# GpSimd's tap additions of a 31-tap causal convolution, issued as 512-column pieces instead of 1024

## The chip, the cores and the metric

The kernel runs on one core of a Trainium2 chip. The metric is the device time of one execution in microseconds (us), lower being better; a kernel's time is the median of its runs. The engines are named as the profile names them: PE (TensorE's matmuls), PEld (its weight loads), DVE (VectorE), ACT (ScalarE), POOL (GpSimd) and SP (the queue from which DMAs are issued).

## The reference

One inference step of a two-layer streaming encoder over 2048 prompt frames and 32 sample frames, model width 1024, in float32. Layer 0 has two branches of 512 channels, layer 1 a token-mixing branch and a stick-breaking attention. The change touches layer 0's branch B, a Conformer convolution module:

```python
proj = xn @ w_in
a_x, a_c, a_b, a_z, b_val, b_glu, b_z = jnp.split(proj, 7, axis=-1)
a_conv, new_a = _causal_dwconv(a_c * a_x, hist_a, a_conv_w)                    # 3 taps
a_out = a_b * a_conv * jax.nn.silu(a_z)
b_conv, new_b = _causal_dwconv(b_val * jax.nn.sigmoid(b_glu), hist_b, b_conv_w) # 31 taps
b_out = jax.nn.silu(_layernorm(b_conv, b_ln_g, b_ln_b)) * jax.nn.silu(b_z)
y = jnp.concatenate([a_out, b_out], axis=-1) @ w_out
```

Each of the 512 channels of branch B is convolved along time with its own 31 taps. All outputs (the streams, the convolution states, keys and values) are float32.

## The kernel before, in words

**Layout.** Features lie on the 128 partitions, time along the columns. The 2080 columns are worked in two halves (1056 with the sample's 32 columns in the first, 1024 in the second), each half in three chunks of 352, 352 and 352 or 320 columns. A branch of 512 channels is four tiles of 128, numbered j.

**Matmuls.** Every float32 product is made of three fp32r products (high x high, high x low, low x high). `split` (lines 172 to 175) makes the two parts: ACT copies the high part (L174), DVE subtracts it from the source (L175). A step of `run_phase` (line 259) is one output tile of one chunk: 24 matmuls into one of three PSUM banks. `wconv` (line 236) splits a tile of weights as two pieces of 512 columns, about one tile for every three steps. The two subtractions L175 (tiles wf, whl) stand behind each other on DVE, and both inputs lie in SBUF.

**Order of the work.** The program's order is fixed when it is built. PE's steps set the pace: four times in each step `tick` (line 145) advances the lanes, queues of generators with a rate each, and what a lane yields between two ticks goes into the engines' queues there. Each engine then works through its own queue in order.

**Layer 0's input phase** (`l0_in`, line 606) runs once for each half, and the convolutions run as lanes beside its 84 steps. The tiles of branch B are shared out. Tiles 1 and 3 are made on DVE (`conv_b_dve`, line 662): one multiply-add per tap over all columns (L672) with the accumulator in PSUM. Tiles 0 and 2 are made by ACT and GpSimd (`conv_b_pool`, line 681): for each tap ACT multiplies the shifted input by the tap's weight into a buffer `cvt` (L692, two buffers), and GpSimd adds the buffer to the tile's row of R (L694). `pieces(30)` (line 657) gives the column ranges: in the first half 1024 columns of the prompt and 32 of the sample, in the second half 1024 columns alone. So the first half has two adds for each tap and the second has one; 30 taps x 2 tiles make 60 taps in each half. ACT's next product into a buffer waits until GpSimd has read it.

**What stands beside it.** DVE also does the short convolution of branch A (`conv_a`, line 699: L704 and L709, all operands in SBUF) and reads most PSUM banks (L747, L761, L771, L775); PE's step three later needs the bank that is read. GpSimd also keeps the convolutions' states (L647, L651), multiplies R by the gate (L773, which waits for DVE's zz, L771), and, when both of its tiles are done, does the sums of branch B's layer norm (`layernorm`, line 793: L801 to L803), for whose result PE's matmul L808 waits.

Of the kernel before, what the change touches and what calls it, by code (L numbers as in the profile page):

```python
# [85 lines left out]
class Build:  # L86
# [519 lines left out]
    def l0_in(self, half):  # L606
        nc, I, O = self.nc, self.I, self.O
        ph = 0 if half == 0 else 3
        R = q = None
# [3 lines left out]
        NP = 1024  # L613

        def begin():
            nonlocal R, q
            if half == 0:
                self.xst.close()
                self.R = self.rst2.enter_context(self.tc.tile_pool(
                    name="l0", bufs=1, side="right", reuse_waits="tile")).tile([P, 8, 1056], F32, name="R0")  # L620
            R = self.R
            q = self.lp = cst.enter_context(self.tc.tile_pool(name="conv", bufs=1, reuse_waits="tile"))
            self.on512 = q.tile([P, P], F32, name="on512")
            nc.gpsimd.memset(self.on512, 1.0 / 512)
            nonlocal dve
            dve = self.lane(0.5, *(conv_b_dve(j) for j in (1, 3)))
            self.lane(0.35, *(conv_b_pool(j) for j in (0, 2)))
            for c in HC[half]:
                self.lane(0.25, ln_b(c, 3 * (c % 3)))
            self.prep(self.prep_sbuf(ph + 1, half, "cat"))  # L630
# [26 lines left out]
        def pieces(hist):  # L657
            if half == 0:
                return [(0, NP, 0), (hist + NP, hist + NP + 32, NP)]
            return [(0, NP, 0)]  # L660
# [20 lines left out]
        def conv_b_pool(j):  # L681
            while ("u", j) not in self.ready:
                yield
            u = U[j]
            n = NP + 62 if half == 0 else NP
            wb = K_CB + 31 * j
            for a, b, d in pieces(30):
                nc.scalar.activation(R[:, 4 + j, d : d + b - a], u[:, a:b], AF.Copy, scale=self.kc[:, wb : wb + 1])
            yield
            for t in range(1, 31):  # L690
                f = q.tile([P, NP + 62], F32, tag="cv", name="cvt", bufs=2)
                nc.scalar.activation(f[:, :n], u[:, t : t + n], AF.Copy, scale=self.kc[:, wb + t : wb + t + 1])  # L692
                for a, b, d in pieces(30):
                    nc.gpsimd.tensor_add(R[:, 4 + j, d : d + b - a], R[:, 4 + j, d : d + b - a], f[:, a:b])  # L694
                yield
            self.ready.add(("conv", j))
            yield
# [927 lines left out]
```

## Time and profile before

| | us |
|---|---|
| median of 3 runs (2697.5 to 2699.49) | 2698.99 |
| the profiled execution | 2703.41 |
| its span | 2701.7 |
| PE busy in the span | 2602.0 (96%) |
| DVE busy | 1712.7 (63%) |
| ACT busy | 1280.8 (47%) |
| POOL busy | 990.7 (37%) |
| the adds L694, 180 of them | 322.4 |

Everything in the profile is of the one profiled execution, whose own time lies 4.4 us above the median of the runs. Busy time is that of an engine's instructions; a busy share over the whole span hides stretches in which an engine is full. A line of the trace that groups instructions gives their count, busy time and mean duration, and then the idle time of the engine just before them and what ended it. A duration holds also the time in which an instruction that has begun is held up. L694 is line 694 of the kernel.

### The profile page before, as it was taken

To read this page: it belongs to the slowest core of one execution; us is meant where nothing else is said; L and a number is where in the kernel's file an instruction comes from. 1 tells how busy PE (TensorE), PEld (TensorE's weight loads), DVE (VectorE), ACT (ScalarE), POOL (GpSimd) and SP (SyncE) were. 2 spreads that over 40 slices of the span, in tenths; PEclk is the share of its full clock that TensorE was granted. 3 is DMA by queue.
4 is the path that set the end of the run, shared out by engine and by line. 5 is a ranking of instruction groups with operands and counts; after the bars stand their busy time and mean duration, and the time that the engine had idled before them with its cause. 6 is when DMAs were issued, how large, how long until landed. Compare 5 with 4: busy or idle time off the path is not lost.

```text
span 2701.7 us, 44677 instructions
## 1 busy us (share of the span) xinstructions
PE 2602.0 (96%) x16738; PEld 2522.4 (93%) x16738; DVE 1712.7 (63%) x2809; ACT 1280.8 (47%) x2348; POOL 990.7 (37%) x883
## 2 busy tenths in 40 slices
PE   7999999999999999999999999998899999998998
PEld 7999999999999999999889999898799899897997
DVE  6697644467986434622242568777788988976344
ACT  5554433445544323432341366666766666753233
POOL 2699712117796001200201044445354343551012
PEclk9999999999999999999999999999999999999998
DMA  5111124331111133455121585543234533324411
GB/s 193 52 45 40 48 85 149 107 111 48 48 43 44 62 106 109 124 197 181 57 78 66 187 250 183 182 128 93 72 95 120 159 109 118 123 83 165 127 60 63
DMA packets 215320, 291.05 MB, mean 108 GB/s; under 512 B 23744, under 2 KB 142144, under 8 KB 215104
## 3 DMA queue, kind: packets, MB, share of 16 engines
q1 hardware_dynamic: 215104, 288.20, 34.0%
q8 instruction: 132, 2.16, 0.3%
q14 instruction: 84, 0.69, 0.1%
HBM read 220.16 MB, written 67.96 MB: 107 GB/s over the span
## 4 chain that ended last, share of the span: by engine, by line
PE 76%; DVE 9%; issue 4%; POOL 4%; DMA 3%; ACT 3%; SPq 1%; DVEq 0%; ACTq 0%; POOLq 0%
PE mm L275 59%; PE o L1249 4%; PE at L1228 4%; POOL R L694 2%; PE ple L287 2%; PE z L1197 2%; PE z L1198 2%; DVE kp L1207 2%; DVE whl L175 1%; DVE op L387 1%; PE mm L534 1%; DMA qt<-qd 1%; PE cm L1058 1%; DVE stg L353 1%; DMA kc<-in_ck 1%
## 5 line engine op out<-in xcount | busy, mean ns | idle before, releaser
L275 PE MATMUL mm<-op,whl 128*128 128x352 f32 (+1 forms) x12672 | 2145.1, 324 | 33.0 <-DVE R L837 8.8
L275 PEld LDWEIGHTS mm<-op,whl 128*128 128x128 f32 x12672 | 2011.7, 189 | 51.1 <-DVE R L837 9.1
L1211 POOL TENSOR_TENSOR bt<-bt,kp 128x512 f32<-128x512 f32 (+2 forms) x320 | 308.0, 965 | 524.9 <-DVE kp L1207 253.1
L175 DVE TENSOR_TENSOR whl<-wf,whl 128x512 fp32r<-128x512 f32 x352 | 304.9, 904 | 154.6 <-ACT whl L174 143.1
L694 POOL TENSOR_TENSOR R<-R,cvt 128x1024 f32<-128x1024 f32 (+1 forms) x180 | 322.4, 1817 | 45.8 <-ACT cvt L692 42.5
L174 ACT CAST whl<-wf 128x512 fp32r<-128x512 f32 x352 | 202.4, 621 | 222.4 <-PE mm L275 176.8
L911 POOL TENSOR_TENSOR acc<-acc,zz 128x352 f32<-128x352 f32 (+1 forms) x78 | 76.8, 984 | 552.5 <-ACT zz L907 552.5
L1203 ACT ACTIVATE kp<-z 128x512 f32<-128x512 f32 (+2 forms) x320 | 171.7, 536 | 223.9 <-PE z L1200 102.3
L1207 DVE TENSOR_TENSOR_SCAN kp<-kp,cr,z 128x513 f32<-128x513 f32 x192 | 245.1, 1277 | 50.3 <-ACT bt L1204 47.9
L692 ACT ACTIVATE cvt<-u,kc 128x1086 f32<-128x1086 f32 (+1 forms) x120 | 140.8, 1178 | 128.1 <-POOL R L694 122.7
L175 DVE TENSOR_TENSOR aT<-at,aT 128x512 fp32r<-128x512 f32 (+1 forms) x288 | 188.7, 656 | 2.0 <-ACT aT L174 2.0
L1249 PE MATMUL o<-aT,vt 128*128 128x256 f32 (+1 forms) x1152 | 185.2, 283 | 0.0
L1228 PE MATMUL at<-ident,bt 128*128 128x128 f32 x1088 | 168.7, 275 | 9.2 <-DVE aT L175 6.2
L1204 ACT ACTIVATE bt<-z 128x512 f32<-128x512 f32 (+2 forms) x320 | 170.1, 532 | 0.0
L174 ACT CAST aT<-at 128x512 fp32r<-128x512 f32 (+1 forms) x288 | 164.5, 571 | 6.9 <-PE at L1228 5.6
L1249 PEld LDWEIGHTS o<-aT,vt 128*128 128x128 f32 x1152 | 164.5, 189 | 0.0
L1228 PEld LDWEIGHTS at<-ident,bt 128*128 128x128 f32 x1088 | 127.5, 141 | 36.5 <-DVE aT L175 7.2
L1207 DVE TENSOR_TENSOR_SCAN kp<-kp,z 128x129 f32<-128x129 f32 (+3 forms) x128 | 104.8, 819 | 84.3 <-ACT bt L1204 83.6
L672 DVE SCALAR_TENSOR_TENSOR acc<-u,kc,acc 128x1086 f32<-128x1086 f32 (+1 forms) x116 | 152.9, 1318 | 2.6
L894 DVE TENSOR_TENSOR sg<-ple,sg 128x352 f32<-128x352 f32 (+1 forms) x72 | 37.1, 515 | 162.0 <-PE ple L287 110.9
L837 DVE TENSOR_TENSOR R<-mm,row 128x352 f32<-128x352 f32 (+1 forms) x96 | 49.5, 516 | 139.9 <-PE mm L275 136.6
L1197 PE MATMUL z<-kt,qt 128*128 128x512 f32 (+2 forms) x320 | 118.3, 370 | 12.7 <-DVE kp L1207 7.7
(188 smaller groups left out, 2218.9 us busy)
## 6 DMA issues: line engine op xcount, KB each, us to landing
wf<-in_win SPq DMA_DIRECT2D x224, 256.0 KB, 3.0
kt<-kd SPq DMA_DIRECT2D x80, 256.0 KB, 4.0
vt<-vd SPq DMA_DIRECT2D x80, 256.0 KB, 3.7
wf<-in_wout SPq DMA_DIRECT2D x64, 256.0 KB, 3.3
wf<-in_wg SPq DMA_DIRECT2D x64, 256.0 KB, 3.1
qt<-qd SPq DMA_DIRECT2D x128, 128.0 KB, 3.4
vd<-vs SPq DMA_DIRECT2D x16, 512.0 KB, 4.3
kd<-hl SPq DMA_DIRECT2D x32, 256.0 KB, 4.0
```

The costliest lines, as they stand in the source:

```text
L174: self.nc.scalar.copy(hi, src)
L175: self.nc.vector.tensor_sub(lo, src, hi.bitcast(F32))
L275: nc.tensor.matmul(ps, wt[:, a, k, :], x[:, b, k, :w], start=(n == 0), stop=(n == 23))
L672: nc.vector.scalar_tensor_tensor(out=acc[:, :n], in0=u[:, t : t + n], scalar=self.kc[:, wb + t : wb + t + 1], in1=acc[:, :n], op0=ALU.mult ...
L694: nc.gpsimd.tensor_add(R[:, 4 + j, d : d + b - a], R[:, 4 + j, d : d + b - a], f[:, a:b])
L1197: nc.tensor.matmul(z[:, :N], qq[:, 0, e * P : e * P + P], kk[:, :N], start=True, stop=False)
L1203: nc.scalar.activation(kp[:, :N], z[:, :N], AF.Sigmoid, scale=-0.125)
L1204: nc.scalar.activation(bt[:, :N], z[:, :N], AF.Sigmoid, scale=0.125)
L1207: nc.vector.tensor_tensor_scan(rev, rev, z[:, 0:1].to_broadcast([P, N + 1]), init, op0=ALU.mult, op1=ALU.bypass)
L1211: nc.gpsimd.tensor_mul(bt[:, :N], bt[:, :N], kp[:, 1 : N + 1])
L1228: nc.tensor.transpose(at[:, off : off + P], bt[:, kb * P : (kb + 1) * P], self.ident)
L1249: nc.tensor.matmul(d, vt[(G, h, c)][:, kb], t[:, l, o0 : o0 + w], start=(c == G and p == 0 and bank == 0 and x == 0 and l == 0), stop=(fin ...
```

## The change

The inner loop of `conv_b_pool` now walks each column range in steps of NP // 2 = 512 columns: the add over 1024 columns becomes two adds over 512, and the 32-column add of the first half stays one. The values added are the same, and ACT's product stays one instruction over all columns. GpSimd has 120 instructions more.

```diff
                 for a, b, d in pieces(30):
-                    nc.gpsimd.tensor_add(R[:, 4 + j, d : d + b - a], R[:, 4 + j, d : d + b - a], f[:, a:b])
+                    for h in range(0, b - a, NP // 2):
+                        e = min(h + NP // 2, b - a)
+                        r = R[:, 4 + j, d + h : d + e]
+                        nc.gpsimd.tensor_add(r, r, f[:, a + h : a + e])
                 yield
```

## Rows read from the trace of the kernel before

**Rows 1.** The page: busy time and share of the span of each engine.
```profile
PE 2602.0 (96%) x16738; PEld 2522.4 (93%) x16738; DVE 1712.7 (63%) x2809; ACT 1280.8 (47%) x2348; POOL 990.7 (37%) x883
```

**Rows 2.** Windows: length; busy PE, PEld, DVE, ACT, POOL; clock; DMA share; GB/s.
```profile
88.00:277.00 189.00, 183.26 (x1131) 182.12 (x1129) 146.79 (x150) 97.93 (x118) 183.24 (x142) 0.99 0.15 46
638.00:807.00 169.00, 161.77 (x1029) 160.99 (x1028) 156.34 (x126) 85.22 (x104) 148.84 (x67) 0.99 0.15 45
```

**Rows 3.** Timeline of PE: start, length, instructions, [idle time before <- what ended it].
```profile
200.44 34.59 PE L275 MATMUL mm<-op,whl 128*128 128x352 f32 x216 [0.63 <-DVE zz L771]
235.77 11.87 PE L275 MATMUL mm<-op,whl 128*128 128x352 f32 x72 [0.74 <-DVE prod L761]
250.71 25.00 PE L275 MATMUL mm<-op,whl 128*128 128x352 f32 x144 [3.07 <-DVE zz L771]
277.02 0.86 PE L808 MATMUL stat<-l,on 128*128 128x352 f32 x2 [1.31 <-POOL l L803]
...
731.43 22.61 PE L275 MATMUL mm<-op,whl 128*128 128x352 f32 x144 [1.06 <-DVE prod L761]
755.92 22.58 PE L275 MATMUL mm<-op,whl 128*128 128x352 f32 x144 [1.88 <-DVE R L775]
782.79 17.46 PE L275 MATMUL mm<-op,whl 128*128 128x352 f32 x100 [4.29 <-DVE prod L761]
```

**Rows 4.** Windows behind two of PE's stops; the granted clock stands third from last.
```profile
250.70:254.10 3.40, 3.39 (x11) 3.39 (x12) 3.40 (x4) 1.25 (x2) 3.37 (x2) 0.51 0.00 0
...
782.80:786.20 3.40, 3.40 (x13) 3.40 (x14) 3.37 (x4) 2.54 (x3) 3.32 (x2) 0.56 0.00 0
```

**Rows 5.** Groups of POOL by shape, 223.9 to 231.3 us: busy us, mean ns.
```profile
L694 POOL TENSOR_TENSOR R<-R,cvt 128x1024 f32<-128x1024 f32 x3 | 7.2, 2404 | 0.0
L694 POOL TENSOR_TENSOR R<-R,cvt 128x32 f32<-128x32 f32 x3 | 0.7, 236 | 0.0
```

**Rows 6.** Timeline of POOL, first half (three taps) and second half (four).
```profile
223.71 7.73 POOL L694 TENSOR_TENSOR R<-R,cvt 128x32 f32<-128x32 f32 x6
...
728.43 9.86 POOL L694 TENSOR_TENSOR R<-R,cvt 128x1024 f32<-128x1024 f32 x4
```

**Rows 7.** Groups of POOL by shape, whole span: the two that work on 512 columns.
```profile
L1211 POOL TENSOR_TENSOR bt<-bt,kp 128x512 f32<-128x512 f32 x224 | 247.4, 1104 | 305.9 <-DVE kp L1207 156.4 <-DVE kp L1188 118.5 <-PE at L1228 15.7
...
L1268 POOL TENSOR_TENSOR fo<-fo,dz 64x512 f32<-64x512 f32 x32 | 41.3, 1290 | 22.6 <-DVE fo L1267 14.9 <-POOL bt L1211 5.1 <-issue 1.2
```

**Rows 8.** Groups of POOL by shape, 90 to 277 us, with the idle time before.
```profile
L694 POOL TENSOR_TENSOR R<-R,cvt 128x1024 f32<-128x1024 f32 x60 | 151.4, 2524 | 9.7 <-ACT cvt L692 9.7
...
L773 POOL TENSOR_TENSOR R<-R,zz 128x352 f32<-128x352 f32 x6 | 8.5, 1423 | 0.9 <-DVE zz L771 0.9
...
L651 POOL COPY keep_a<-prod 128x2 f32<-128x2 f32 x3 | 1.0, 349 | 1.4 <-DVE prod L761 1.4
```

**Rows 9.** Timeline of POOL: the first tap of the first half.
```profile
88.78 4.97 POOL L694 TENSOR_TENSOR R<-R,cvt 128x1024 f32<-128x1024 f32 x3 [7.21 <-ACT cvt L692]
```

**Rows 10.** Timeline of DVE: weight splits with POOL idle, in each half, and between them.
```profile
819.84 1.29 DVE L175 TENSOR_TENSOR whl<-wf,whl 128x512 fp32r<-128x512 f32 x2 [2.70 <-ACT whl L174]
...
110.03 1.44 DVE L175 TENSOR_TENSOR whl<-wf,whl 128x512 fp32r<-128x512 f32 x2 [1.68 <-ACT whl L174]
...
761.55 5.16 DVE L175 TENSOR_TENSOR whl<-wf,whl 128x512 fp32r<-128x512 f32 x2
...
766.64 7.90 DVE L672 SCALAR_TENSOR_TENSOR acc<-u,kc,acc 128x1024 f32<-128x1024 f32 x6
774.45 5.34 DVE L175 TENSOR_TENSOR whl<-wf,whl 128x512 fp32r<-128x512 f32 x2
```

**Rows 11.** Groups of DVE by shape: 638 to 807 us, then 88 to 277 us.
```profile
L175 DVE TENSOR_TENSOR whl<-wf,whl 128x512 fp32r<-128x512 f32 x28 | 56.7, 2062 | 0.2 <-ACT whl L174 0.2
...
L672 DVE SCALAR_TENSOR_TENSOR acc<-u,kc,acc 128x1086 f32<-128x1086 f32 x58 | 78.3, 1350 | 1.3
```

**Rows 12.** Groups of POOL by shape, 638 to 807 us: the gate's product.
```profile
L773 POOL TENSOR_TENSOR R<-R,zz 128x352 f32<-128x352 f32 x4 | 5.7, 1437 | 7.3 <-DVE zz L771 7.3
```

## The prediction, made before the change was run

> **What bounds the kernel now.** I read the page first, then the windows, then PE's timeline, then GpSimd and VectorE in the two stretches where L694 runs. On the page PE is busy for 2602.0 us of the span [rows 1], so an edit on GpSimd can only give or take the time in which PE stands still or runs at the lower clock. L694 runs in two stretches, one for each half of the sequence: 88 to 277 us and 638 to 807 us. In them GpSimd is busy for 183.24 of 189 and 148.84 of 169 us, VectorE for 146.79 and 156.34 [rows 2]. So GpSimd is full in the first half, and VectorE nearly full in the second.
>
> PE's timeline shows seven stops there [rows 3]. In the first half they are 0.63 + 0.74 + 3.07 + 1.31 = 5.75 us. The last of them, at 277.02, waits for GpSimd itself (L803, the sums of the layer norm, which stand in GpSimd's queue right behind the last tap). That wait settles the first half: whatever PE lost earlier, it reaches 277 ahead of GpSimd and waits for it. In the second half there are three stops, 1.06 + 1.88 + 4.29 = 7.23 us, and all three wait for VectorE to read a PSUM bank (L761, L775). [...]
>
> **The change, part by part.**
>
> *Price of a tap on GpSimd.* A 1024-column add takes 2.404 us and a 32-column one 0.236 where nothing disturbs them [rows 5]. Three undisturbed taps of the first half, six instructions, fill 7.73 us [rows 6], and their durations sum to 3 x (2.404 + 0.236) = 7.92: at each of five joints the next instruction starts 0.04 us before the last one ends. In the second half, where each add needs the one just before it, four adds of 2.405 fill 9.86 us: (9.86 - 2.41) / 3 = 2.483 from start to start, a gap of 0.08. So an add pays 0.08 when it depends on its neighbour and gains 0.04 when it doesn't. After the change the neighbour is always the other half of the columns (or the 32), so every joint is of the cheap kind.
>
> No 512-column add of this line exists. The nearest rows are L1268, 1.290 us for 64x512, and L1211, 1.104 for 128x512 [rows 7]. The line through this kernel's own adds (0.236 at 32 columns, 2.404 at 1024) gives 0.236 + 480 x 2.168 / 992 = 1.285, and I take that, since L1268 agrees; 1.104 stays as the lower bound. A first-half tap then goes from 2.404 to 2 x 1.285 - 0.04 = 2.53, so +0.126 us; a second-half tap from 2.483 to 2 x 1.285 - 2 x 0.04 = 2.49, so nothing. With 1.104 a first-half tap would be 0.24 cheaper; with no overlap at the new joint, 0.166 dearer. The reported durations alone would say 2 x 1.285 - 2.405 = +0.165 for every tap of both halves, +9.9 us each; I go by the spacing. [...]
>
> *First half: a cost on the path.* 60 taps [rows 8] x 0.126 = +7.6 us on a full engine. GpSimd's idle time takes up part: 9.7 us are put down to waits for ACT's cvt, of which 7.2 lie before the first tap [rows 8, 9], which leaves 2.5; 1.4 ahead of L651 and 0.9 ahead of L773. All these are waits for work that follows PE or VectorE, so a later GpSimd finds its data ready: up to 4.8 us are absorbed. L803 then ends 7.6 - 4.8 = 2.8 us later (none absorbed: 7.6), and with it PE's stop at 277. PE comes to that stop earlier than now, for its waits on VectorE shorten, so the stop grows past 3 us and should be followed by a dip like those of [rows 4]; this one stands behind the last wait for GpSimd, where nothing hides it: +1.7. First half: +4.5 us, between 0 and +9.
>
> *VectorE's wait for GpSimd.* The weight split (L175, two subtractions of 512 columns in a row) takes 1.29 us for the pair with GpSimd idle [rows 10]. In the second half one subtraction takes 2.062 on average, 28 times [rows 11], and single pairs 5.16 and 5.34 us [rows 10]: each subtraction waits until the 1024-column add that is running has ended, and GpSimd's next add waits for the subtraction. In the first half a pair can take 1.44 [rows 10], since there the short 32-column add is the one that gets in between. L672, whose accumulator lies in PSUM, keeps 1.350 under a GpSimd that never rests [rows 11], so only L175 and the additions of the short convolution are concerned. With 512 columns the wait is at most 1.29 in place of 2.4. A pair of the second half, arriving at random: 0.64 + 0.65 + 1.29 + 0.65 = 3.2 us in place of 5.2.
>
> *Second half: a gain on the path.* From 761.55 to 779.79, three microseconds ahead of the longest stop's end, VectorE has no pause [rows 10]; the two pairs inside give 5.16 + 5.34 - 6.4 = 4.1 us of the 4.29, and the pairs before them pay for the rest. The stops at 731 and 756 have the same cause. What is late next is GpSimd: if PE runs 7.23 + 1.7 = 8.9 us ahead of now, GpSimd must as well, and it has the room, 7.3 us of waiting ahead of L773 for VectorE's zz [rows 12], which shrinks with VectorE's delay. It is 1.6 short, partly covered by PSUM's three banks. I take 0.9 off: -8.0, between -4 and -8.9.
>
> *Sum.* +4.5 - 8.0 = -3.5 us. The profiled execution took 2703.4 (span 2701.7); it becomes 2699.9. The median of the runs, 2699.0, lies 4.4 below the profiled one, so I give 2695.5. No DMA is added or moved. On GpSimd's queue stand, behind the adds, L651, L647, L773 and the layer norm; they shift with the sums above.
>
> **The rivals.**
>
> *A. The first half pays nothing (0.25).* The idle time and VectorE's shorter waits take up all of the cost, or a 512 add costs nearer to 1.104. Then the second half's -8.0 stands alone: 2691; at 1.104 the first half's own 5.75 + 1.7 go too: 2683. For it: three stops of the first half also end on VectorE [rows 3]. Against it: GpSimd rests for 5.8 of 189 us [rows 2], and the last stop is on GpSimd.
>
> *B. VectorE gains nothing (0.10, slower).* The second half of a tap is queued and overlaps the first by 0.04; if GpSimd keeps hold of what both need across that joint, VectorE waits for both halves, 2.5 us as now. Then the second half keeps its 7.23 + 1.7 and the first pays +4.5: 2703.5, and 2708 if nothing is absorbed. It decides if a pair in the second half still takes 5 us. Against it: joints of the same kind, 1024 to 32 in the first half, let a subtraction in, or the pair at 110.03 could not take 1.44 [rows 10]. [...]
>
> *C. GpSimd bounds the second half too (0.10).* If the waits ahead of L773 don't shrink, PE can gain only what PSUM's banks allow: about the first two stops, -2.9, and with the first half's +4.5 the time is 2700.6.
>
> **How the numbers follow.** The forecast has 0.55, A 0.25, B 0.10, C 0.10. A measurement of this kernel can tell some 0.2%, 5.4 us, from no change: faster is below 2693.6, slower above 2704.4. The forecast's own range is 2691 to 2700 (its halves' bounds don't all fall together), about a quarter of it below 2693.6: 0.14, with A's 0.22 faster has 0.36. Slower is half of B and a little of C and of the forecast: 0.08. The rest, 0.56, is no change. The range reaches to A's upper part and B's lower end: 2688 to 2703.
>
> **What would show it.** L694's 512-column adds near 1.285 us, starting some 0.04 before the last one ends. L175 in the second half at 1.3 to 1.5 on average, from 2.062. PE's stops of 731, 756 and 783 gone or below 1 us, and the dip at 783 with them. The stop ahead of L808 at 277 still on GpSimd's L803, longer than 1.31, ending 2 to 4 us later, with a dip behind it. The forecast is wrong if L175's mean stays near 2 (B), if the stop at 277 ends no later than now (A), or if stops of the second half end on GpSimd or ACT (C).

## The result, and the profile after

The changed kernel takes 2725.99 us in the median against 2699.49 before. One run of each (3273.33 and 3177.78 us), and one of e4 below (3624.74), was disturbed: it counts in the medians and in no range or ratio, and without it the two medians lie 22.2 us apart instead of 26.5. The changed kernel's range is 2710.39 to 2728.33. The ratio is 1.0079 with an interval of 1.0064 to 1.0093. By the ratio that is 21 us. 2695.5 was forecast, 3.5 us faster, in a range of 2688 to 2703: the kernel is slower than the whole range. The profiled execution took 2716.96 (span 2715.2), 9 less than the median. Lines behind the edit stand three lower in the changed kernel: L697 is L694, L750 is L747, L764 is L761, L774 is L771, L806 is L803, L811 is L808, L825 is L822. L175 and L672 stand before the edit.

The page of the changed kernel, busy time of each engine, against [rows 1]:
```profile
PE 2598.7 (96%) x16738; PEld 2520.2 (93%) x16738; DVE 1738.1 (64%) x2809; ACT 1280.7 (47%) x2348; POOL 1006.2 (37%) x1003
```
GpSimd has its 120 instructions more and is busy 15.5 us longer. VectorE has not one instruction more, and is busy 25.4 us longer. That is the row to follow.

PE's timeline in the two stretches, its stops alone, against [rows 3]: start, length, instructions, [idle time before <- what ended it].
```profile
128.76 48.62 PE L275 MATMUL mm<-op,whl 128*128 128x352 f32 x288 [10.45 <-DVE u L750]
178.62 69.86 PE L275 MATMUL mm<-op,whl 128*128 128x352 f32 x432 [1.25 <-DVE prod L764]
256.73 36.42 PE L275 MATMUL mm<-op,whl 128*128 128x352 f32 x216 [8.24 <-DVE prod L764]
295.61 0.86 PE L811 MATMUL stat<-l,on 128*128 128x352 f32 x2 [2.47 <-POOL l L806]
...
732.35 46.34 PE L275 MATMUL mm<-op,whl 128*128 128x352 f32 x288 [6.09 <-DVE prod L764]
778.95 22.74 PE L275 MATMUL mm<-op,whl 128*128 128x352 f32 x144 [0.26 <-DVE R L778]
802.74 11.39 PE L275 MATMUL mm<-op,whl 128*128 128x352 f32 x72 [1.04 <-DVE prod L764]
816.40 20.76 PE L275 MATMUL mm<-op,whl 128*128 128x352 f32 x120 [2.27 <-DVE zz L774]
```
The layer norm's matmul is reached at 295.61 instead of 277.02: 18.6 us of the loss lie in the first half. Its four stops make 22.4 us where there were 5.75. The two long ones, of 10.45 and 8.24 us, are new and wait for VectorE to read a PSUM bank. In the second half the stops make 9.7 us where 7.23 were. Windows around the three longest, from inside each stop to some microseconds behind it, show what follows (length; busy PE, PEld, DVE, ACT, POOL; granted clock; DMA share; GB/s):
```profile
120.80:134.50 13.70, 5.74 (x20) 5.75 (x21) 13.60 (x11) 2.34 (x3) 4.92 (x5) 0.50 0.13 39
...
250.50:261.00 10.50, 4.27 (x15) 4.28 (x16) 10.43 (x8) 4.63 (x5) 8.51 (x11) 0.51 0.15 50
728.40:735.20 6.80, 2.85 (x10) 2.86 (x11) 6.76 (x8) 2.56 (x4) 1.72 (x2) 0.50 0.26 77
```
Around each stop PE is granted half its clock (0.50, 0.51 and 0.50). In the kernel before PE did 11 matmuls in the 3.40 us at 0.51 [rows 4] and 22 in the 3.40 us behind them, at 0.99. By that, the 5.74, 4.27 and 2.85 us that it works at the lower clock cost about half of themselves, by estimate 2.9, 2.1 and 1.4. First half: 22.4 - 5.75 + 2.9 + 2.1 - 1.7 (the dip of before, by the same estimate half of the 3.40 us of [rows 4]) = 20, which covers the 18.6. At the last of the layer norm's matmuls (L825, 878.77 against 856.31) the changed kernel is 22.5 us behind; from there to the end its profile is 9.0 shorter than that of before (1836.4 and 1845.4 us), in work that the change doesn't touch, so the spans differ by 13.5 alone.

What VectorE does ahead of the three stops at 128.76, 256.73 and 732.35 stands in its timeline:
```profile
110.77 14.85 DVE L175 TENSOR_TENSOR whl<-wf,whl 128x512 fp32r<-128x512 f32 x2 [2.09 <-ACT whl L174]
...
236.44 8.29 DVE L672 SCALAR_TENSOR_TENSOR acc<-u,kc,acc 128x1086 f32<-128x1086 f32 x6
244.64 8.95 DVE L175 TENSOR_TENSOR whl<-wf,whl 128x512 fp32r<-128x512 f32 x2
...
705.99 13.72 DVE L175 TENSOR_TENSOR whl<-wf,whl 128x512 fp32r<-128x512 f32 x2
719.64 7.90 DVE L672 SCALAR_TENSOR_TENSOR acc<-u,kc,acc 128x1024 f32<-128x1024 f32 x6
```
and GpSimd beside it:
```profile
109.86 6.90 POOL L697 TENSOR_TENSOR R<-R,cvt 128x512 f32<-128x512 f32 x8
116.71 0.12 POOL L644 MEMSET u<- 128x30 f32 x1
116.78 8.94 POOL L697 TENSOR_TENSOR R<-R,cvt 128x512 f32<-128x512 f32 x9
134.89 0.70 POOL L651 COPY keep_b<-u 128x30 f32<-128x30 f32 x1 [9.16 <-DVE u L750]
...
235.91 14.64 POOL L697 TENSOR_TENSOR R<-R,cvt 128x32 f32<-128x32 f32 x16
...
703.54 15.03 POOL L697 TENSOR_TENSOR R<-R,cvt 128x512 f32<-128x512 f32 x12
724.58 2.52 POOL L697 TENSOR_TENSOR R<-R,cvt 128x512 f32<-128x512 f32 x2 [6.02 <-ACT cvt L692]
```
A pair of subtractions that takes 1.29 us alone [rows 10] takes 14.85, 8.95 and 13.72, and each time GpSimd has been going from instruction to instruction without a rest. The single subtraction that begins at 705.99 is let in only when GpSimd runs out of work at 703.54 + 15.03 = 718.57, and ends at 719.11. The L672, whose accumulator lies in PSUM, take no part in this: beside the adds that run without a rest from 235.91 to 250.55 six of them take 8.29 us, and their mean over the first half is 1.350 us as before [rows 11].

The group L175 in the changed kernel, the same two stretches as before (88 to 277, 638 to 807): the first two lines with min/median/max in ns, the others with busy us and mean ns.
```profile
L175 DVE TENSOR_TENSOR whl<-wf,whl x29: 678/925/11770, 87.4 to 276.5; 128x512 fp32r<-128x512 f32 x29
L175 DVE TENSOR_TENSOR whl<-wf,whl x28: 677/1439/13122, 638.2 to 798.0; 128x512 fp32r<-128x512 f32 x28
...
L175 DVE TENSOR_TENSOR whl<-wf,whl 128x512 fp32r<-128x512 f32 x29 | 55.5, 1950 | 13.1 <-ACT whl L174 13.0
L175 DVE TENSOR_TENSOR whl<-wf,whl 128x512 fp32r<-128x512 f32 x28 | 50.8, 1854 | 14.4 <-ACT whl L174 14.4
```
In the second half the median falls to 1.439 us, but the mean, forecast at 1.3 to 1.5, falls only to 1.854 (from 2.062 in [rows 11]), because of single waits of up to 13 us. A mean that stays near 2 is the sign that the prediction named for rival B. In the first half, where the mean had been 0.896, it is 1.950.

I counted **joints** in the trace: the end of a GpSimd instruction at which an L175 or a multiply-add of the short convolution (L712) that has begun is still held up, and the next GpSimd instruction follows without a pause. At such a joint VectorE is either let in (GpSimd's next instruction then takes longer: the 32-column add beside which the subtraction of 11.77 us ends takes 0.730 us, against 0.236 in [rows 5]) or passed over. In the kernel before it was passed over at none; in the changed one at 47. The counts are good to some joints: with other bounds for "held up" these two become 0 or 1 and 40 to 53. The subtraction of 11.77 us was passed over at 13 joints in a row, that of 13.12 at 10.

Why a wait ends shows in the waits between 704 and 726 us (engine, line <- what it waited for: us in total, times, longest):
```profile
ACT whl L174 <- DMA wf<-in_win: 6.6, 2, 6.3
POOL R L697 <- ACT cvt L692: 6.0, 1, 6.0
...
SPq L229 <- DVE whl L175: 21.2, 2, 21.0
```
The load of the next weights (L229) waits for L175 to have read the buffer; ACT's copy L174 waits for the load; the products for GpSimd stand behind L174 in ACT's queue. So here the held subtraction starves GpSimd in the end, and only that pause lets VectorE in. It is not the only way out: the subtraction of 11.77 us was let in at a joint and ended at 122.54, while GpSimd added on until 125.72. By 719 us VectorE is 13 us behind with PSUM reads still to come in its queue, and PE then stands for them.

### The profile page after: what moved, and what is told of

Its sections match the earlier page's. It is cut to its first block, busy times and chain, and to the rows that moved or that the text cites. A ratio compares the mean times of both kernels' runs of the same rounds, so it can differ in the third digit from the quotient of the medians.

```text
span 2715.2 us, 44857 instructions
## 1 busy us (share of the span) xinstructions
PE 2598.7 (96%) x16738; PEld 2520.2 (93%) x16738; DVE 1738.1 (64%) x2809; ACT 1280.7 (47%) x2348; POOL 1006.2 (37%) x1003
## 5 line engine op out<-in xcount | busy, mean ns | idle before, releaser
L175 DVE TENSOR_TENSOR whl<-wf,whl 128x512 fp32r<-128x512 f32 x352 | 334.1, 987 | 149.2 <-ACT whl L174 137.9
L697 POOL TENSOR_TENSOR R<-R,cvt 128x512 f32<-128x512 f32 (+1 forms) x300 | 341.4, 1175 | 48.0 <-ACT cvt L692 48.0
L174 ACT CAST whl<-wf 128x512 fp32r<-128x512 f32 x352 | 202.7, 621 | 232.9 <-PE mm L275 162.0
L175 DVE TENSOR_TENSOR aT<-at,aT 128x512 fp32r<-128x512 f32 (+1 forms) x288 | 188.6, 655 | 2.0 <-ACT aT L174 2.0
L174 ACT CAST aT<-at 128x512 fp32r<-128x512 f32 (+1 forms) x288 | 164.9, 573 | 7.2 <-PE at L1231 6.0
L672 DVE SCALAR_TENSOR_TENSOR acc<-u,kc,acc 128x1086 f32<-128x1086 f32 (+1 forms) x116 | 152.8, 1318 | 2.6
```

The lines of the kernel that those rows point to most:

```text
L174: self.nc.scalar.copy(hi, src)
L175: self.nc.vector.tensor_sub(lo, src, hi.bitcast(F32))
L672: nc.vector.scalar_tensor_tensor(out=acc[:, :n], in0=u[:, t : t + n], scalar=self.kc[:, wb + t : wb + t + 1], in1=acc[:, :n], op0=ALU.mult ...
L697: nc.gpsimd.tensor_add(r, r, f[:, a + h : a + e])
```

## The experiments

Theory 1: GpSimd can pass VectorE over when its next add needs nothing of the adds that have just run; an add that needs the one right before it lets VectorE in. Against it stand the higher price on GpSimd (more instructions, more joints), the mere number of pieces, and chance at each joint. All kernels keep everything but the loop of the adds. A ratio is to runs of the kernel before beside the experiment's own, whose medians are 2700.31 to 2701.50 for e1 to e11. "First" and "second" are L175's mean and longest in us, in the stretches 88 to 277 and 638 to 807; "passed" counts the joints of both halves at which VectorE was passed over. L175's times and the joints are of one profiled run each.

| kernel | median us (range) | ratio to before | first: mean, longest | second: mean, longest | passed |
|---|---|---|---|---|---|
| before | 2699.49 | 1 | 0.90, 2.90 | 2.06, 2.90 | 0 |
| changed | 2725.99 (2710.4 to 2728.3) | 1.0079 [1.0064, 1.0093] | 1.95, 11.77 | 1.85, 13.12 | 47 |
| e1, first half cut | 2723.18 (2715.4 to 2731.2) | 1.0084 [1.0054, 1.0113] | 1.74, 6.53 | 2.10, 2.91 | 24 |
| e2, second half cut | 2704.04 (2691.7 to 2708.3) | 1.0007 [0.9992, 1.0021] | 1.20, 2.91 | 1.48, 6.33 | 7 |
| e3, one column shared | 2711.94 (2708.9 to 2715.8) | 1.0043 [1.0028, 1.0058] | 1.00, 1.78 | 1.50, 1.82 | 0 |
| e4, second half 992 + 32 | 2693.44 (2691.0 to 2700.2) | 0.9972 [0.9960, 0.9983] | 0.90, 2.04 | 1.13, 2.82 | 2 |
| e5, turning order | 2707.90 (2703.4 to 2710.3) | 1.0022 [1.0013, 1.0031] | 1.21, 1.79 | 1.37, 1.79 | 2 |
| e6, turning, first half whole | 2701.17 (2696.1 to 2706.4) | 0.9999 [0.9988, 1.0010] | 1.24, 2.91 | 1.41, 1.86 | 2 |
| e7, second half 4 x 256 | 2731.60 (2728.2 to 2734.5) | 1.0115 [1.0098, 1.0132] | 0.90, 2.90 | 3.23, 15.47 | 66 |
| e8, second half 768 + 256 | 2704.89 (2696.1 to 2717.5) | 1.0013 [0.9995, 1.0030] | 0.89, 2.57 | 2.25, 13.80 | 19 |
| e9, only second half turning | 2694.80 (2692.4 to 2703.6) | 0.9983 [0.9972, 0.9994] | 0.87, 1.42 | 1.38, 1.87 | 1 |
| e10, second half 496 + 32 + 496 | 2716.43 (2707.2 to 2721.2) | 1.0057 [1.0038, 1.0077] | 0.91, 2.40 | 2.02, 11.78 | 34 |
| e11, second half 896 + 128 | 2707.59 (2691.6 to 2713.2) | 1.0018 [1.0000, 1.0036] | 1.01, 2.88 | 1.66, 8.44 | 10 |

**Each half alone (e1, e2).** The edit of e1; e2 has half == 1 in it.
```diff
+                    W = NP // 2 if half == 0 else NP
+                    for h in range(0, b - a, W):
+                        e = min(h + W, b - a)
```


> Only the first half's 1024-column adds are cut in two; the second half keeps one add per tap. Theory 1 (long waits: 512-column adds that don't need the add just before them follow each other so closely that a subtraction L175 can be passed over at joint after joint): the first half shows single L175 of 4 us and more, mean about 2 us against 0.90 before, and the stop ahead of L808 ends 10 to 20 us later than 277; the second half shows no L175 over 3 us, mean about 2.06; time 2707 to 2722. Theory 2 (price: the time is that of 60 more adds on a full GpSimd): no L175 over 3 us in either half, L808 about 3 to 8 us later, time 2702 to 2707.

> Only the second half's adds are cut in two; the first half keeps its 1024 and 32 columns. Theory 1: the first half shows no L175 over 3 us; in the second most L175 take 1.0 to 1.8 us, but one to three of them wait for several adds (4 to 13 us) and stop PE for 3 us and more behind them; time 2693 to 2710, unsteady from run to run. Theory 2: no L175 over 1.9 us in the second half, all three stops gone, time 2690 to 2693.

The first half alone gives the whole loss: 1.0084, with PE stops of 3.08 and 8.93 us there that wait for VectorE, and the second half as before (mean 2.10). Its median lies 1 us above what theory 1 gave. The second half alone comes to no measurable difference, although its L175 mean falls from 2.06 to 1.48. What takes the gain back isn't shown: e2's profile is of its fastest run (2691.72), in which the one wait of 6.33 us makes none of the PE stops of 3 us and more that theory 1 expected in the second half (the longest is 2.25 us), and of its slower runs, up to 2708.25, there is no profile.

**An add that needs its neighbour (e3).** The first pieces reach one column into the second:
```diff
+                        e = min(h + W, b - a)
+                        e = min(e + 1, b - a)
```


> Both halves cut in two, but the first piece reaches one column into the second (0 to 513, 512 to 1024), so that column 512 gets each tap twice, and the second piece needs the first and the next tap's first piece needs the second piece. Theory 1: a joint with such a need leaves the gap of 0.08 us that the joints of the second half had before, and every subtraction gets in there: no L175 over 2.2 us in the second half, mean 1.2 to 1.5; in the first half none over 3 us. GpSimd pays 0.12 us more for such a joint: about 15 us more work in each half than the two-piece version, so the time is 2698 to 2712, but steadier. Theory 2: as the pieces are as many and the joints dearer, the time is above that of the changed kernel, 2730 and more. Theory 3 (each joint lets the subtraction in by chance, whether the adds need each other or not): single L175 of 4 us and more remain.

L175 in both stretches (min/median/max ns):
```profile
L175 DVE TENSOR_TENSOR whl<-wf,whl x28: 680/752/1783, 98.5 to 267.8; 128x512 fp32r<-128x512 f32 x28
L175 DVE TENSOR_TENSOR whl<-wf,whl x28: 680/1774/1816, 644.3 to 800.2; 128x512 fp32r<-128x512 f32 x28
```
As many instructions as in the changed kernel, one column more in each of the first pieces, and no wait passes 1.82 us: at most the rest of one add and its own time. VectorE is passed over at no joint. Theory 1's numbers came, and not the higher time of theory 2 or the long waits of theory 3. The time is still 1.0043: now GpSimd pays at each joint (it rests 4.3 us in all ahead of its 55 adds of 512 columns between 638 and 807 us, 0.08 each), and PE waits 6.28 us for its sums ahead of the layer norm's matmul, which comes at 288.97.

**Order alone (e5, e6, e9).** The pieces of the changed kernel, in turning order:
```diff
+                W = NP // 2
+                cuts = [(a + h, min(a + h + W, b), d + h) for a, b, d in pieces(30) for h in range(0, b - a, W)]
+                for a, b, d in cuts if t % 2 else cuts[::-1]:
```


> The same 512-column pieces in both halves, and all values added are those of the changed kernel; only the order turns at each tap: left, right (and the 32 columns), then (32,) right, left. At every second joint (every third in the first half) the next add now needs the add just before it. Theory 1 (an add that needs its neighbour lets VectorE in; one that doesn't may pass it over): no L175 longer than about 3.3 us (two adds of 1.29 and its own 0.64), lost joints only at the independent ones, at most one in a row; L175's mean 1.0 to 1.6 us in both halves. A first-half tap is 2 x 1.285 + 0.236 with joints of +0.08, -0.04, -0.04, or about 2.81 us against 2.69 in the changed kernel, so GpSimd ends the first half some 7 us later than it would there without the passing over: 2703 to 2712. Rival (the number of pieces alone makes VectorE lose, whatever needs what): waits of 6 us and more as in the changed kernel, mean near 2, 2718 to 2732.

L175 in both stretches of e5:
```profile
L175 DVE TENSOR_TENSOR whl<-wf,whl x28: 682/1168/1789, 98.7 to 265.8; 128x512 fp32r<-128x512 f32 x28
L175 DVE TENSOR_TENSOR whl<-wf,whl x28: 683/1570/1790, 642.4 to 795.1; 128x512 fp32r<-128x512 f32 x28
```
The same instructions with the same operands as in the changed kernel, in another order, and the longest wait falls from 13.12 to 1.79 us, the time from 1.0079 to 1.0022 of that before. So neither the number of pieces nor their price makes the long waits and the bulk of the loss. e5 is still 0.2% slower than before, with a wait of 5.56 us for GpSimd's sums in the first half. What no run separates is the need itself from the gap of 0.08 us that it leaves between two adds [rows 6]: either could be what lets VectorE in.

> First half as before, second half in the turning order with 512 columns. Theory 1: no second-half L175 over 3.3 us, mean 1.2 to 1.5 (the cut in plain order had 1.49 with one of 6.33 in its profile), at most one lost joint in a row; the runs lie closer together than the 16.5 us of the plain order; 2689 to 2696. Rival (number of pieces alone): as the plain order, 2700 to 2708 with a spread over 12 us. A second rival (with 512 columns the cost lies elsewhere, in joints of 0.08 us and start-up): 2699 to 2704 without long waits.

e6 did not do what its text says: with one piece of 1024 the list of the first half was turned as well (1024, 32, then 32, 1024). The layer norm's matmul came at 283.24 instead of 277.02 there (in e2, whose first half is that of before, at 277.13). It says nothing of the second half alone; e9 does:
```diff
+                W = NP // 2 if half == 1 else NP
...
+                for a, b, d in cuts if half == 0 or t % 2 else cuts[::-1]:
```


> The kernel of the run before with this order turned its first half too (1024, 32 | 32, 1024), against its intention: there GpSimd's long adds stood next to each other at every second tap and L808's stop came 6 us later. Here the first half keeps the plain order and 1024 + 32, and only the second half turns, in 512 columns. Theory 1: first half as before (L808 at 277, L175's mean near 0.9), second-half L175 at 1.4 to 1.5 with none over 2 us, PE's second-half stops some 4.5 us in sum without a dip, against 7.2 and a dip of 1.7: 2694 to 2699, ratio 0.997 to 0.999. Rival (the second half gains nothing from shorter waits, since GpSimd or ACT takes the place of VectorE there): 2700 to 2703.

0.9983, inside what theory 1 gave: with the waits bounded, cutting the second half does gain, by the ratio 4.6 us, near the lower bound of what the prediction gave the second half (4 to 8.9).

**Other cuts of the second half (e4, e7, e8, e10, e11).** The edit of e4 (for its 992 e7 has NP // 4, e8 768 and e11 896), and then that of e10:
```diff
+                W = 992 if half == 1 else NP
...
+                cuts = pieces(30) if half == 0 else [(0, 496, 0), (496, 528, 496), (528, NP, 528)]
```


> The first half as before; the second half's add is cut into 992 and 32 columns, the pattern that the first half has had all along (1024 and 32). Theory 1: what let VectorE in there is that a tap's long add needs the long add two places ahead of it, so that no more than one add stands ready; no L175 over 3.2 us, a pair in the second half at about 2.0 to 2.6 us (mean of one 1.0 to 1.3), its stops of 1.06, 1.88 and 4.29 us gone; GpSimd pays 0.02 us a tap; time 2689 to 2694, below both kernels. Theory 3: with the joints overlapping, single L175 wait for several adds, time 2697 or more. Theory 2: time within 2 us of before.

> First half as before, second half in four pieces of 256 columns, plain order, so that an add needs the one four back. Line through the 32- and 1024-column adds: 0.236 + 224 x 2.168 / 992 = 0.726 us, a tap 4 x (0.726 - 0.04) = 2.74 us against 2.48, +15.6 us on GpSimd in a half where it rested some 20. Theory 1 with skew (the longer the stretch of adds that need nothing recent, the more often VectorE is passed over): several runs of lost joints, longest wait 5 us or more, L175's mean 1.3 to 2.2, 2702 to 2712. Rival (each joint lets VectorE in with the same chance, so shorter pieces mean shorter waits): mean under 1.2, no wait over 3 us, and the time set by GpSimd alone, 2694 to 2702.

> First half as before, second half in pieces of 768 and 256 columns, plain order. A tap costs GpSimd about 1.845 + 0.726 - 0.08 = 2.49 us, as before. 992 + 32 had 2 lost joints and 2693.4, 512 + 512 had 7 lost in its profile and 2704. Theory 1 with skew (what counts is how long the piece is that stands between an add and the one it needs: 0.24, 0.73 and 1.29 us): lost joints and time in between, 2 to 6 lost, 2693 to 2702. Rival (any independent neighbour will do, the 32-column piece is a special case): 7 or more lost, 2702 to 2708. Rival (only equal pieces lose): no more than 2 lost, 2690 to 2694.

> First half as before; second half in pieces of 496, 32 and 496 columns, plain order, so that no add needs either of the two just before it. A tap costs GpSimd 2 x 1.250 + 0.236 - 3 x 0.04 = 2.62 us against 2.48, +8 us where it rested 20. It asks why 992 + 32 let VectorE in. Theory 1 (an add with no need of a recent add can pass VectorE over; in 992 + 32 the long add needs the one 0.24 us back): lost joints in rows, waits over 4 us, L175's mean 1.5 to 2.2, 2700 to 2715. Rival (a 32-column add is what lets VectorE in, whatever needs what): VectorE gets in at every 32-column add, no wait over 2 us, mean near 1.1, 2691 to 2698.

> First half as before; second half in pieces of 896 and 128 columns, plain order. The 128-column add takes about 0.446 us by the line through the 32- and 1024-column adds, and stands between each long add and the one it needs: 0.24 us there gave 2 lost joints and 2693.4, 0.73 us (768 + 256) gave 19 lost, waits of 13.8 us and 2704.9. Theory 1, if the distance back in time counts: between them, 2 to 15 lost, 2693 to 2704. Rival (0.24 us was a special case of the shortest piece): as 768 + 256, 15 or more lost and waits over 10 us. Rival (something between 0.45 and 0.73 us decides): 2 or fewer lost, 2690 to 2695.

VectorE's and then GpSimd's timeline of e7 (its L696 is L694):
```profile
698.83 16.07 DVE L175 TENSOR_TENSOR whl<-wf,whl 128x512 fp32r<-128x512 f32 x2
```
```profile
694.29 19.47 POOL L696 TENSOR_TENSOR R<-R,cvt 128x256 f32<-128x256 f32 x28
719.62 2.78 POOL L696 TENSOR_TENSOR R<-R,cvt 128x256 f32<-128x256 f32 x4 [5.87 <-ACT cvt L692]
```
Pieces half as long make it worse: 28 adds in a row, a pair of subtractions of 16.07 us, let in when GpSimd pauses at 713.76. The rival of an equal chance at each joint wanted waits under 3 us and is out. So is the rival that a 32-column add lets VectorE in by itself: in e10, with such an add in every tap, 34 joints pass and a subtraction takes 11.78 us.

In the profiles these kernels fall in order by the closest need in a tap: how long the pieces take that stand between an add and the one that it needs. For the long add that is 0.24 us (32 columns, by [rows 5]), 0.45 (128) and 0.73 (256; both estimates by the line through [rows 5]), 1.29 (512 and 512), 1.49 (e10) and three times 0.73 (e7). Passed joints: 2, 10, 19, then 7 (e2) and 34, and 66. Only e2 stands out of the row; the second half of the changed kernel, in the same pieces, has two to three times as many. Each count is of one run: e2's and e7's profiles are of their fastest, e8's and e11's of runs near their slowest. The times bear out less than the row: e4 (0.9972) is faster than e11, e8 and e2 (1.0018, 1.0013, 1.0007), which can't be told apart, and e10 and e7 are slower. In e10 and e7 the need also lies three and four adds back instead of two, and GpSimd has more work, so there the time since the need isn't separated from these. In this form the theory covers what its first one doesn't: the 32-column add of e4 needs an add that ended over 2 us ago, and still VectorE is let in ahead of it, as it is in e5 at over 30 joints at which the next instruction doesn't wait for its neighbour. One close need in each tap or two seems to keep the other joints open; that fits the runs and is not shown by itself. For e7 the theory had the direction, and a time far too low (2702 to 2712); for e8 it gave 2 to 6 passed joints and 19 came, and for e11 a time up to 2704 where 2707.6 came. The times of e8 (2704.9, up to 2702 expected) and e10 (2716.4, up to 2715) came out high as well.

**e4 beats both kernels.** PE's stops of the second half in e4 (its L775 is L771), against the last three of [rows 3]:
```profile
789.67 7.90 PE L275 MATMUL mm<-op,whl 128*128 128x352 f32 x48 [2.62 <-DVE zz L775]
798.33 11.41 PE L275 MATMUL mm<-op,whl 128*128 128x320 f32 x72 [0.77 <-DVE zz L775]
```
3.4 us in place of 7.23, L175's mean at 1.13 us, and 0.9972 of the time before, 7.5 us less.

## Why the prediction was wrong

**The price of the adds: right, within 0.02 us a tap.** In the changed kernel's first half, between 220 and 236 us, a 512-column add takes 1.291 us on average; 1.285 was predicted. ACT's products follow GpSimd's taps one for one where VectorE is passed over:
```profile
111.38 1.21 ACT L692 ACTIVATE cvt<-u,kc 128x1086 f32<-128x1086 f32 x1
114.09 1.21 ACT L692 ACTIVATE cvt<-u,kc 128x1086 f32<-128x1086 f32 x1 [1.50 <-POOL R L697]
116.80 1.21 ACT L692 ACTIVATE cvt<-u,kc 128x1086 f32<-128x1086 f32 x1 [1.50 <-POOL R L697]
```
2.71 us a tap from start to start, against (7.73 - 0.04) / 3 = 2.56 before [rows 6]: +0.15, and +0.126 was predicted. In the second half the twelve adds in 15.03 us above make (15.03 - 1.28) / 11 = 1.25 from start to start, 2.50 a tap, and 2.49 was predicted.

**VectorE's wait: the step that failed.** "With 512 columns the wait is at most 1.29 in place of 2.4" holds only if GpSimd lets VectorE in at every joint. The median wait of the changed kernel keeps to it; the mean is set by the others. The step counted the new joint as one "of the cheap kind" and took the saving of 0.08 + 0.04 us for pure gain; e3, with no joint passed, and e5, with no L175 over 1.79 us, show that the dear joint, at which an add waits for its neighbour, is the one at which VectorE was let in every time.

**The dismissal of rival B.** B had the direction: GpSimd keeps VectorE waiting across overlapped joints, 47 of them in the changed kernel; what it would keep hold of there is shown by no run. I gave it 0.10 because joints of 1024 to 32 let a subtraction in [rows 10]. That reading was right, and the conclusion was not: there the long add needs an add from which only the 32-column one, 0.24 us, parts it, as in e4, and at such joints VectorE is seldom passed over (2 in e4). It says nothing of an add with 1.29 us and more between it and its need. B was also priced too low. It let GpSimd keep its hold for one tap, 2.5 us "as now", and so gave 2703.5 to 2708; the trace shows a hold over up to 13 joints, and nothing in the sum bounded that.

**First half.** +4.5 us were forecast, from GpSimd's price. It is +18.6. Windows of before [rows 2] and of after:
```profile
88.00:296.00 208.00, 185.58 (x1128) 184.34 (x1127) 175.25 (x149) 96.95 (x116) 189.12 (x202) 0.94 0.13 39
```
GpSimd is busy 5.9 us longer (7.6 predicted) in a stretch that is 19 longer, and rests 18.9 us where it rested 5.8. The step that GpSimd's idle time would absorb 4.8 us has the wrong sign: L651 stands in GpSimd's queue and waits for VectorE's reads, and its wait of 9.16 us ahead of 134.89 is the late subtraction's doing. "Whatever PE lost earlier, it reaches 277 ahead of GpSimd" came true in the letter, PE still waits 2.47 us for GpSimd there; but it took GpSimd's time for free of PE's and VectorE's, and the reads for which PE stood 10.45 and 8.24 us kept GpSimd waiting too.

**Second half.** -8.0 was forecast; from 629.29 to the matmul at 878.77 (611.03 and 856.31 before) the stretch is 4.2 us longer. The stops of 731 and 756 went, that of 783 shrank to 1.04, and one of 6.09 came at 732.35 with a granted clock of 0.50 around it. The step from shorter waits to a shorter second half holds: in e4 and e9, where no L175 of the second half takes more than 2.82 and 1.87 us, the kernel gains 7.5 and 4.6 us. No run shows the 1.7 us that the sums of both halves take for a dip, an estimate, half of the 3.40 us of [rows 4]: for 3.4 us behind the stops at 295.61, where the sums add it, and at 802.74 (783 before), where they take it off, the granted clock is 1.00; it is 0.50 or 0.51 in the windows around the three longest stops, and 0.50 from 817.1 to 820.5.

## What to carry to other kernels

Before you cut a long GpSimd instruction so that VectorE gets in more often, look at what each piece needs: here, pieces that needed nothing recent kept a VectorE subtraction with both inputs in SBUF out for up to 15.47 us, until GpSimd paused (e7). Keep the need close, by a short second piece (992 + 32: no L175 of that half over 2.82 us in e4) or by turning the order at each step (none over 1.87 us in e9), and read the longest duration of the waiting group beside its mean and median. Where a joint is cheap, ask who used the pause.

## What the runs showed of the hardware that was not expected

- A VectorE subtraction with both inputs in SBUF was passed over at 13 joints in a row (11.77 us) and at 10 (13.12 us), though it had begun before each of the adds that went ahead.
- In single profiles, the longer ago the needed add ended, the more often GpSimd passes VectorE over: from 2 joints at 0.24 us to 66 at three adds of 0.73, with e2 (7 at 1.29) out of the row. Where the two pieces of a tap share a column (e3), at none. What causes the row is shown by no run.
- Two kernels in which VectorE is passed over scatter widely: ten runs of e8 reach over 21.4 us and ten of e11 over 21.6, ten of e5 (turning order) over 7.0. It is no rule: four runs of e7, with 66 passed joints, reach over 6.3, and 24 of the kernel before over 13.3.
- A wait of VectorE ended through its own damage in the changed kernel: the held L175 keeps the next weights from being loaded (L229 waits 21.0 us for it), ACT stands at L174 (6.3 us), and GpSimd's next product is late by 6.0 us.
